# Four of eight experts in 96 places: 64 as column halves, 32 on four column tiles, plain float32 weights

## The chip, the cores and the metric

One core of one Trainium2 chip runs the kernel in one launch. The metric is device time in microseconds (us), the median of several runs. The engines are TensorE (PE; PEld is its weight load), VectorE (DVE), ScalarE (ACT), GpSimd (POOL) and SyncE (SP), whose queue issues the weight transfers.

## The reference, cut to what matters

A two-layer encoder trunk over 256 positions of width 1024, in float32. The change touches only the last sub-layer, in which each position goes through two of eight SwiGLU experts, 3584 wide:

```python
def moe_swiglu(h, w_router, w_gate, w_up, w_down):
    logits = (h @ w_router).astype(jnp.float32)
    top_v, top_i = lax.top_k(logits, TOP_K)          # 2 of 8
    gates = jax.nn.softmax(top_v, axis=-1)
    dense_gate = jnp.sum(jax.nn.one_hot(top_i, N_EXPERTS) * gates[..., None], axis=-2)
    y = jnp.zeros_like(h)
    for e in range(N_EXPERTS):
        y = y + dense_gate[..., e:e + 1] * swiglu(h, w_gate[e], w_up[e], w_down[e])
    return y
```

With the reference's own inputs its router gives the eight experts 70, 71, 46, 62, 84, 71, 66 and 42 positions.

## The kernel before, in words

Weights come from HBM in pieces of 128 partitions x 1024 floats (512 KB), issued by SP in one fixed order into a pool of `NW` = 34 such buffers. `Stream` keeps the account: `load` issues a transfer, `fill` issues as many as buffers allow (`NW - ROOM` alive at once), `step` turns a piece that is not marked `RAW` into two float32r pieces, `hi` (ACT, line 193) and `lo` = raw - hi (DVE, line 194), and `get` hands the pieces of a unit out, one k-slice at a time, ahead of the products that use them.

In the expert stage the experts are sorted by their number of positions. Rank 0 is always expert 0; ranks 1 to 7 are the others, smallest first. They are worked through in the order of `RANKS` = (0, 1, 7, 6, 2, 5, 4, 3). An expert's columns come in seven slices of 512 (`NFE`), and each slice has a gate product (`pg`), an up product (`pu`), both over 8 k-slices, and a down product (`y`), over 4 k-slices and two output halves. There are two forms:

- Ranks 0, 4, 5, 6, 7 hold 128 places. Each weight is split, and `mm3` (lines 362 to 364) issues three float32r products in place of one: hi x hi, hi x lo, lo x hi. A slice has 72 of them, 128 columns of TensorE and 512 moving elements wide: 24 for gate, 24 for up, 24 for down.
- Ranks 1, 2, 3 (`SMALL`) hold `PLACES` = 64 places. Their weights stay raw, and the products are plain float32, which show in the trace as two records (passes) each. TensorE's array is used as two column tiles of 64: two slices are taken at a time, one on each half (`halves_of`; lines 1158, 1190). A step is thus two slices, and the seventh slice a step of its own whose halves are 256 elements wide.

The main loop (from line 1338 on) issues for each step: gate, `Silu` on ACT (line 1382), up, the multiplication on DVE (line 1384), and then the down product of the step before. All engines run in the order of the program. Smaller work is put into this order by beats: `st.soon(n, fn)` calls `fn` after n more pieces were handed out. So come in between the products: the transposes of the activation (`act_T`, line 1169), the gather of the next expert's rows (`gather`, line 1080, from `expert_in`), the transposed selection matrix `ohT` (line 1126), and, once an expert is done, `expert_out` and four pieces of `scatter` (line 1237), two products each for the hi and lo part of the result, and one addition on DVE.

If an expert had more positions than places, an `overflow` branch behind the loop would work them off.

Of the kernel before, what the change touches and what calls it, by code (L numbers as in the profile page):

```python
# [21 lines left out]
P = 128  # L22
D = 1024
KD = D // P
# [11 lines left out]
SMALL = (1, 2, 3)  # L36
PLACES = 64
EXPERT = 12 * NFE
WINDOWS = (2, 4, 8, 16)
# [12 lines left out]
def trunk_(es, tc, stream, experts, blocks, x, xT, c, columns, ada_w, ln_g, ln_b, ev_w_in, pool_w, ev_sink, ev_w_out,  # L52
# [277 lines left out]
    def expert_units(stage, step):  # L330
        s, fs = step
        r = RANKS[s]
        if stage < 2:
            ks, what = [[(f * 12 + stage * 4 + u, 2) for u in range(4)] for f in fs], None
        elif fs[-1] == NFE - 1:

            ks, what = [[(fs[0] * 12 + 8 + n * 2 + u, 2) for u in range(2)] for n in range(2)], None
        else:
            ks, what = [[(f * 12 + 8 + u, 1) for u in range(4)] for f in fs], None
        if r in SMALL:  # L340
# [101 lines left out]
    with ExitStack() as ph:  # L442
# [423 lines left out]
        for g in range(1, NG):  # L866
            ffn_gu(g)
            if g == 1:
                at_once(next_x(z, affine_rows(0, 0)))

                earlier = cst.tile([P, NE, NE], F32, name="earlier")
                G.iota(earlier, pattern=[[1, NE], [-1, NE]], base=0, channel_multiplier=0, allow_small_or_imprecise_dtypes=True)
                G.tensor_scalar(earlier, earlier, 0.0, None, op0=ALU.is_gt)

                G.iota(upto, pattern=[[1, P]], base=0, channel_multiplier=-1, allow_small_or_imprecise_dtypes=True)
                G.tensor_scalar(upto, upto, 0.0, None, op0=ALU.is_ge)
                slot = cst.tile([P, P], F32, name="slot")
# [3 lines left out]
                G.memset(places[:, SMALL[0]:SMALL[-1] + 1], float(PLACES))  # L881
            if g == NG - 1:
# [179 lines left out]
    with ExitStack() as ph:  # L1062
# [27 lines left out]
        def expert_in(s, res):  # L1090
# [4 lines left out]
            here = (mA, mB)[s % 2]  # L1095
            if small:
                h = here.tile([P, KD, PLACES], F32, tag="hh", name="hs")
# [4 lines left out]
            res[:] = h, ohT  # L1102
            yield 10
            for q in range(2):
                sl = slice(q * 4, q * 4 + 4)
                ps = gather(oh, q, PLACES if small else P)
                yield 1
                if small:
                    affine(h[:, sl, :], ps, q)
                    yield 10  # L1110
                    continue
# [7 lines left out]
            if s == NE - 1:  # L1119
                ungated, oh = oh, m1.tile([P, NT, P], F32, tag="oh", name="og", bufs=2)  # L1120
                for t in range(NT):
                    V.tensor_scalar(oh[:, t, :], ungated[:, t, :], gate_by[:, t, r:r + 1], None, op0=ALU.mult)
                yield 2
            ps = pst.tile([P, 512], F32, tag="t", name="pso")
            for t in range(NT):
                T.transpose(ps[:, t * P:(t + 1) * P], oh[:, t, :], ident)
            yield 1
            A.activation(ohT, ps[:, 0:S], AF.Copy)

        def by_halves(stages):  # L1130
# [9 lines left out]
        def up_gate(step, h, ps):  # L1140
# [18 lines left out]
            for _ in ws:  # L1159
                pass  # L1160

        def act_T(step, act, res):

# [14 lines left out]
        def down(step, aT, y):  # L1178
            s, fs = step
            small = RANKS[s] in SMALL  # L1180
            if fs[-1] == NFE - 1:
                for n in range(2):
                    down_half(step, aT, y, n)
            elif small:
                ws = st.get()
                for kk in range(4):
                    pair = [next(ws) for _ in range(2)]
                    for n in range(2):
                        for rows_, w in zip(halves_of, pair):
                            T.matmul(y[n][rows_, :], lhsT=aT[0][:, kk, rows_], rhs=w[:, n * 512:(n + 1) * 512],  # L1190
                                     start=fs[0] == 0 and kk == 0, stop=False)
                for _ in ws:
                    pass
# [8 lines left out]
        def down_half(step, aT, y, n):  # L1202

            ws = list(st.get())
            if RANKS[step[0]] in SMALL:
                for k in range(2):
                    for b, rows_ in enumerate(halves_of):
                        T.matmul(y[n][rows_, :], lhsT=aT[0][:, k, rows_], rhs=ws[b * 2 + k], start=False, stop=k == 1)  # L1208
            else:
                for k, w in enumerate(ws):  # L1210
                    mm3(y[n], sl2(aT, lambda a: a[:, k, :]), w, False, k == 3)

        def expert_out(y, res):

            yhl = last8.tile([P, 2, D], F32R, tag="d", name="yhl")
            yh, yl = yhl[:, 0, :], yhl[:, 1, :]
            res[:] = yh, yl
            sls = [slice(n * 512, n * 512 + 512) for n in range(2)]
            yf = last4.tile([P, D], F32, tag="r", name="yf")
# [3 lines left out]
            for sl in sls:  # L1223
                A.activation(yh[:, sl], yf[:, sl], AF.Copy)
                yield 1
            for sl in sls:
                V.tensor_tensor(yl[:, sl], yf[:, sl], yh[:, sl], op=ALU.subtract)
                yield 1

        def scatter(r, ohT, ys):  # L1230

            for t in range(NT):
                for n in range(2):
                    sl = slice(n * 512, n * 512 + 512)
                    ps = pst.tile([P, 512], F32, tag="t", name="pssc")
                    for i, yy in enumerate(ys):
                        T.matmul(ps, lhsT=ohT[:, t * P:(t + 1) * P], rhs=yy[:, sl], start=i == 0,
                                 stop=i == len(ys) - 1)
                    yield 1
# [23 lines left out]
        def overflow(r, base):  # L1263
# [3 lines left out]
            for q in range(2):  # L1267
                affine(h2[:, q * 4:q * 4 + 4, :], gather(oh, q), q)
            y = [psa.tile([P, 512], F32, tag="b", name="y2") for _ in range(2)]
            for f in range(NFE):  # L1270
                gu = []
                for w in range(2):
# [5 lines left out]
                    gu.append(ps)  # L1278
                act = m2.tile([P, 512], F32, tag="act", name="act2")
                A.activation(act, gu[0], AF.Silu)  # L1280
# [31 lines left out]
        cur = [None, None]  # L1312
        at_once(expert_in(0, cur))
        by_rank = cst.tile([P, 6, NE], F32, name="by_rank")
        pos_by, gate_by = by_rank[:, 0:2, :], by_rank[:, 2:4, :]
# [36 lines left out]
        for i, step in enumerate(steps):  # L1352
# [10 lines left out]
            if step == (0, (5,)):  # L1363
                cnt = nc.values_load(found[:, NE:NE + 1], min_val=0, max_val=S)
                by_halves(next_x(z, rows10))
            if (s, fs[0]) == (1, 2):
                for t in range(NT):
# [4 lines left out]
            aT = [None, None]  # L1372
            n = 256 if RANKS[s] in SMALL and len(fs) == 1 else 512
# [7 lines left out]
            act = m2.tile([P, 512], F32, tag="act", name="act")  # L1381
            A.activation(act[:, 0:n], pg[:, 0:n], AF.Silu)  # L1382
            up_gate(step, h, pu)
            V.tensor_tensor(act[:, 0:n], act[:, 0:n], pu[:, 0:n], op=ALU.mult)  # L1384
            st.soon(1 if final else 2 if n == 256 else 6, lambda step=step, act=act, aT=aT: by_halves(act_T(step, act, aT)))
            if prev is not None:
                pstep, paT, pohT = prev
                if pstep[1][0] == 0:
                    y = [psy.tile([P, 512], F32, tag="y", name="y") for _ in range(2)]
                down(pstep, paT, y)  # L1390
                if pstep[1][-1] == NFE - 1:
# [7 lines left out]
        with tc.If(cnt > 0):  # L1399
            for r in range(NE):  # L1400
                for base in (PLACES, PLACES + P) if r in SMALL else (P,):
                    overflow(r, base)
# [3 lines left out]
        halves = [slice(n * 512, n * 512 + 512) for n in range(2)]  # L1406
        yf = [m2.tile([P, 512], F32, tag="act", name="yf") for _ in range(2)]
        s6 = [sml.tile([P, 2, 6], F32, tag="s6", name="s6") for _ in range(NT)]
# [100 lines left out]
```

## Time and profile before

| | us |
|---|---|
| median of 3 runs (lowest, highest) | 1317.96 (1314.96, 1318.4) |
| the profiled execution's own time | 1321.59 |
| its span, first to last instruction | 1319.8 |
| PE busy / DVE busy / ACT busy | 1284.6 / 923.1 / 664.7 |
| HBM read | 468.05 MB, 355 GB/s over the span |

The expert stage begins at about 440 us and ends at about 1305 us. A busy TensorE says little here: products are pipelined, the busy time of one covers the start of the next, and so the pace is read from the starts of successive records in the timeline.

### The profile page before, as it was taken

Reading aid. Unit: us, or ns where it says so; the run is one execution under the profiler, and the core shown is the slowest. Engines: PE = TensorE matmul, PEld = TensorE weight load, DVE = VectorE, ACT = ScalarE, POOL = GpSimd, SP = SyncE. Lnnn points to the kernel's source line nnn. Section 1 sums busy time; section 2 is a strip of 40 time slices with the busy share of each in tenths; the row PEclk is TensorE's granted clock in tenths of the full one; section 3 lists DMA queues with packets and bytes.
Section 4 is the critical chain, followed back from the end, with each engine's and each line's share of the span. In section 5 each row is a group of like instructions: output and inputs, shape, how many; then the busy total and the mean of one; then the engine's idle time right before and its main releaser. Section 6 shows DMA issues by size and latency. Waiting matters only on the chain. (4 is left out here: it accounts for less than half of the span.)

```text
span 1319.8 us, 19031 instructions
## 1 busy us (share of the span) xinstructions
PE 1284.6 (97%) x6392; PEld 930.2 (70%) x6392; DVE 923.1 (70%) x1140; ACT 664.7 (50%) x840; POOL 15.5 (1%) x73
## 2 busy tenths in 40 slices
PE   6999999999999999999999999999999999999996
PEld 4758999996976788544688888854467888886332
DVE  7696999947865989312888898842089889975302
ACT  0416353526326777212678777832177777774100
POOL 1000000000000000000000000000000000000001
PEclk9999999999899999999999999999999999999998
DMA  9999899993782889999999999999999999999993
GB/s 372 408 409 367 302 346 356 366 350 129 265 339 106 285 304 347 392 409 409 409 408 409 409 409 353 337 387 409 408 409 409 409 409 409 350 330 372 410 409 142
DMA packets 129579, 470.46 MB, mean 356 GB/s; under 512 B 14520, under 2 KB 14656, under 8 KB 129472
## 3 DMA queue, kind: packets, MB, share of 16 engines
q1 hardware_dynamic: 129168, 468.89, 92.2%
q8 instruction: 52, 0.85, 0.3%
q14 instruction: 55, 0.45, 0.1%
q10 hardware_dynamic: 304, 0.27, 0.1%
HBM read 468.05 MB, written 1.05 MB: 355 GB/s over the span
## 5 line engine op out<-in xcount | busy, mean ns | idle before, releaser
L194 DVE TENSOR_TENSOR lo<-raw,hi 128x1024 fp32r<-128x1024 f32 x494 | 590.4, 1222 | 108.1 <-ACT hi L193 85.1
L193 ACT ACTIVATE hi<-raw 128x1024 fp32r<-128x1024 f32 x494 | 502.7, 1054 | 146.1 <-PE y L364 20.9
L269 DVE CUSTOM_DVE_ANT_0 raw<-raw,cond,colt 128x1024 f32<-128x1024 f32 x96 | 118.7, 1281 | 7.8 <-DMA raw<-in_stream 7.8
L363 PE MATMUL pu<-lo,hh 128*128 128x512 f32 x280 | 111.3, 397 | 1.2 <-DVE over L1344 1.0
L362 PE MATMUL y<-hi,ah 128*128 128x512 f32 x280 | 112.3, 401 | 0.0
L364 PE MATMUL y<-hi,al 128*128 128x512 f32 x280 | 111.0, 397 | 1.1 <-DVE al L1176 1.1
L362 PE MATMUL pu<-hi,hh 128*128 128x512 f32 x280 | 111.5, 398 | 0.0
L363 PE MATMUL y<-lo,ah 128*128 128x512 f32 x280 | 111.0, 396 | 0.1
L364 PE MATMUL pu<-hi,hl 128*128 128x512 f32 x280 | 111.0, 396 | 0.0
L362 PE MATMUL pg<-hi,hh 128*128 128x512 f32 x272 | 110.7, 407 | 0.0
L363 PE MATMUL pg<-lo,hh 128*128 128x512 f32 x272 | 107.9, 397 | 0.7 <-DVE lo L194 0.7
L364 PE MATMUL pg<-hi,hl 128*128 128x512 f32 x272 | 107.7, 396 | 0.0
L1384 DVE TENSOR_TENSOR act<-act,pu 128x512 f32<-128x512 f32 (+1 forms) x47 | 31.3, 666 | 100.0 <-PE pu L1158 92.4
L1174 ACT ACTIVATE ah<-psT 128x512 fp32r<-128x512 f32 (+2 forms) x47 | 27.1, 578 | 133.6 <-PE psT L1169 133.3
L362 PE MATMUL psgu<-hh,hi 128*128 128x256 f32 x320 | 90.3, 282 | 0.0
L364 PE MATMUL psgu<-hh,lo 128*128 128x256 f32 x320 | 90.1, 282 | 0.0
L363 PE MATMUL psgu<-hl,hi 128*128 128x256 f32 x320 | 89.6, 280 | 0.0
L1158 PE MATMUL pu<-raw,hs 128*64 128x512 f32 (+1 forms) x384 | 76.6, 542 | 0.0
L1158 PE MATMUL pg<-raw,hs 128*64 128x512 f32 (+1 forms) x384 | 75.8, 542 | 0.0
L1382 ACT ACTIVATE act<-pg 128x512 f32<-128x512 f32 (+1 forms) x47 | 27.4, 583 | 84.6 <-PE pg L1158 62.3
L1190 PE MATMUL y<-raw,ah 128*64 128x512 f32 x288 | 66.4, 597 | 0.2 <-DMA raw<-in_experts 0.2
L363 PEld LDWEIGHTS pu<-lo,hh 128*128 128x128 f32 x280 | 52.7, 188 | 14.9 <-DVE over L1344 1.4
(274 smaller groups left out, 1822.8 us busy)
## 6 DMA issues: line engine op xcount, KB each, us to landing
raw<-in_experts SPq DMA_DIRECT2D x668, 512.0 KB, 10.1
raw<-in_stream SPq DMA_DIRECT2D x204, 512.0 KB, 7.9
lng<-in_ln_g SPq DMA_DIRECT2D x4, 512.0 KB, 7.5
lnb<-in_ln_b SPq DMA_DIRECT2D x4, 512.0 KB, 8.3
xT<-in_xT SPq DMA_DIRECT2D x2, 512.0 KB, 7.7
x<-in_x SPq DMA_DIRECT2D x2, 512.0 KB, 10.2
guest<-in_experts SPq DMA_DIRECT2D x2, 512.0 KB, 10.1
guests<-in_experts SPq DMA_DIRECT2D x2, 512.0 KB, 6.9
```

The lines of the kernel that those rows point to most:

```text
L193: A.activation(hi, raw, AF.Copy)
L194: V.tensor_tensor(lo, raw, hi, op=ALU.subtract)
L269: V.tensor_tensor_reduce(raw[:, 0, :], raw[:, 0, :], cond, 1.0, adab[:, i:i + 1], ALU.mult, ALU.add, accum_out=mod[l, part][:, kk:kk + 1])
L362: T.matmul(ps, lhsT=l[0], rhs=r[0], start=start, stop=False)
L363: T.matmul(ps, lhsT=l[0], rhs=r[1], start=False, stop=False)
L364: T.matmul(ps, lhsT=l[1], rhs=r[0], start=False, stop=stop)
L1158: T.matmul(ps[rows_, 0:w.shape[-1]], lhsT=h[:, kk + k, :], rhs=w, start=kk + k == 0, stop=kk + k == KD - 1)
L1174: A.activation(ah[:, 0:n, :], ps[:, 0:n, :], AF.Copy)
L1190: T.matmul(y[n][rows_, :], lhsT=aT[0][:, kk, rows_], rhs=w[:, n * 512:(n + 1) * 512], start=fs[0] == 0 and kk == 0, stop=False)
L1382: A.activation(act[:, 0:n], pg[:, 0:n], AF.Silu)
L1384: V.tensor_tensor(act[:, 0:n], act[:, 0:n], pu[:, 0:n], op=ALU.mult)
```

## The change

Ranks 4 to 7 (`MIDDLE`) get 96 places, and take the raw form with two slices per step. Their first 64 places go as those of the small experts do, on two column tiles of 64. The other 32 (`MORE`) go on four column tiles of 32, which take the two slices of up and the two of gate at once (`pm`), and in the down product two slices times two output halves (`ym`). All four weight pieces of a step's k-pair are drawn ahead of its products. Their activation is transposed apart (`psTm`), and their result, whose four blocks have to be summed, is scattered by two further products per piece with two selection matrices `ohM` (`more` times `quarters`). Rank 0 stays as it was. The pool of weight buffers shrinks from 34 to 30.

```diff
+MIDDLE = (4, 5, 6, 7)
+MORE = 32
...
-    NW = 34
+    NW = 30
...
+        if r in MIDDLE and stage < 2:
+            if stage == 0:
+                st.add_expert(r, [(f * 12 + w * 4 + u, 2) for u in range(4) for w in range(2) for f in fs], RAW)
+            return
...
-             (((0, 1), (2, 3), (4, 5), (6,)) if RANKS[s] in SMALL else [(f,) for f in range(NFE)])]
+             (((0, 1), (2, 3), (4, 5), (6,)) if RANKS[s] in SMALL + MIDDLE else [(f,) for f in range(NFE)])]
...
+        def both(step, h, pg, pu, pm):
+            s, fs = step
+            ws = st.get()
+            for kk in range(0, KD, 2):
+                w = [next(ws) for _ in range(4 * len(fs))]
+                for k in range(2):
+                    if len(fs) == 2:
+                        g, u = (w[k], w[2 + k]), (w[4 + k], w[6 + k])
+                    else:
+                        g, u = ((a[:, 0:S], a[:, S:2 * S]) for a in (w[k], w[2 + k]))
+                    n = g[0].shape[-1]
+                    flags = dict(start=kk + k == 0, stop=kk + k == KD - 1)
+                    for ps, pair in ((pg, g), (pu, u)):
+                        for rows_, a in zip(halves_of, pair):
+                            T.matmul(ps[rows_, 0:n], lhsT=h[:, kk + k, 0:PLACES], rhs=a, **flags)
+                    for b, a in enumerate(u + g):
+                        T.matmul(pm[b * MORE:(b + 1) * MORE, 0:n], lhsT=h[:, kk + k, PLACES:], rhs=a, **flags)
...
+        def act_T_both(step, act, actm, res):
...
+            for k in range(n):
+                T.transpose(ps[:, k, :], act[:, k * P:(k + 1) * P], ident)
+            yield 1
+            A.activation(ah[:, 0:n, :], ps[:, 0:n, :], AF.Copy)
...
+            for k in range(n):
+                T.transpose(ps[:, k, :], actm[0:2 * MORE, k * P:(k + 1) * P], ident[0:2 * MORE, 0:2 * MORE])
+            yield 1
+            V.tensor_copy(am[:, 0:n, :], ps[:, 0:n, :])
...
+        def down_more(am, k, b, w, y, first, last):
+            for n, a in w:
+                q = b * 2 + n
+                T.matmul(y[q * MORE:(q + 1) * MORE, :], lhsT=am[:, k, b * MORE:(b + 1) * MORE], rhs=a, start=first, stop=last)
...
+                    if RANKS[s] in MIDDLE:
+                        for b, w in enumerate(pair):
+                            down_more(aT[1], kk, b, [(n, w[:, n * 512:(n + 1) * 512]) for n in range(2)], y[2],
+                                      fs[0] == 0 and kk == 0, False)
...
         def down_half(step, aT, y, n):
...
+                    if RANKS[step[0]] in MIDDLE:
+                        for b in range(2):
+                            down_more(aT[1], k, b, [(n, ws[b * 2 + k])], y[2], False, k == 1)
...
         def scatter(r, ohT, ys):
...
+                    oT, oM = ohT if isinstance(ohT, tuple) else (ohT, None)
+                    ops = [(oT, yy[:, sl]) for yy in ys[:2]]
+                    if oM is not None:
+                        ops += [(oM[:, n, :], ys[2][:, i, :]) for i in range(2)]
...
-            pu = psa.tile([P, 512], F32, tag="b", name="pu")
+            pu = psa.tile([P, 512], F32, tag="b", name="pu", bufs=1)
...
+            elif RANKS[s] in MIDDLE:
+                pm = psa.tile([P, 512], F32, tag="a", name="pm")
+                both(step, h, pg, pu, pm)
...
+            if RANKS[s] in MIDDLE:
+                actm = m2.tile([P, 512], F32, tag="act", name="actm", bufs=3)
+                half = slice(0, 2 * MORE)
+                A.activation(actm[half, 0:n], pm[2 * MORE:, 0:n], AF.Silu)
+                V.tensor_tensor(act[:, 0:n], act[:, 0:n], pu[:, 0:n], op=ALU.mult)
+                V.tensor_tensor(actm[half, 0:n], actm[half, 0:n], pm[half, 0:n], op=ALU.mult)
+                st.soon(2 if n == 256 else 4, lambda step=step, act=act, actm=actm, aT=aT: by_halves(act_T_both(step, act, actm, aT)))
```

How the change moves TensorE's work shows in the order of its instructions. In the gate product of rank 7's second slice (the third expert in line), TensorE has before, with the transposes of the first slice's activation (`psT`) put in between:

```order
L362 MATMUL pg<-hi,hh 128x512
L363 MATMUL pg<-lo,hh 128x512
L364 MATMUL pg<-hi,hl 128x512
L1169 MATMUL psT<-ident,act 128x128 x4
L362 MATMUL pg<-hi,hh 128x512
```

The first three rows make one k-slice of one slice's gate, and all of it is 128 columns wide. At the same place, in the first and second step of rank 7, TensorE now has (`64x512` and `32x512` are 64 and 32 columns of the array; the `y` rows are the last down products of the small expert before):

```order
L1207 MATMUL pm<-raw,hs 32x512 x4
L1285 MATMUL y<-raw,ah 64x512 x4
L1219 MATMUL psT<-ident,act 128x128 x4
L1285 MATMUL y<-raw,ah 64x512 x4
L1224 MATMUL psTm<-ident,actm 128x64 x4
L1205 MATMUL pg<-raw,hs 64x512 x2
L1205 MATMUL pu<-raw,hs 64x512 x2
L1207 MATMUL pm<-raw,hs 32x512 x4
L1205 MATMUL pg<-raw,hs 64x512 x2
L1205 MATMUL pu<-raw,hs 64x512 x2
L1207 MATMUL pm<-raw,hs 32x512 x4
```

One k-slice of gate and up, for two slices of columns, is now two pairs at 64 columns and four products at 32, and with each k-slice the tile goes from 64 to 32 and back. What is put in between is 128 columns wide, or, for `psTm`, 64 rows. In the down product of rank 7's first step there stands, from the end of the scatter of the expert before on:

```order
L1331 MATMUL pssc<-yhl,ohT 128x512 x2
L1263 MATMUL y<-raw,ah 64x512 x4
L1233 MATMUL ym<-raw,am 32x512 x4
L1263 MATMUL y<-raw,ah 64x512 x4
L1233 MATMUL ym<-raw,am 32x512 x4
L1219 MATMUL psT<-ident,act 128x128 x4
L1088 MATMUL psg<-oh,z 128x96 x8
L1224 MATMUL psTm<-ident,actm 128x64 x4
L1263 MATMUL y<-raw,ah 64x512 x4
L1233 MATMUL ym<-raw,am 32x512 x4
```

The same alternation, once per k-slice, takes the place of the down rows `L362 MATMUL y<-hi,ah 128x512` and their two fellows. Over the whole program the shape of TensorE's tile changes 88 times from one product to the next before, and 512 times now: 192 times from 64 to 32 columns, 160 times straight back, and 160 times otherwise.

## Rows read from the trace of the kernel before

**Rows 1.** TensorE, DMA and clock by stretch of the expert stage: us, busy (xinstructions), PEclk, DMA share, GB/s.
```profile
core 0: us, PE busy (x) PEld busy (x) DVE busy (x) ACT busy (x) POOL busy (x), PEclk, DMA share, GB/s
...
629.00:656.00 27.00, 26.93 (x118) 19.26 (x117) 21.97 (x23) 19.37 (x21) 0.00 (x0) 1.00 1.03 409
...
710.00:737.00 27.00, 27.00 (x129) 22.07 (x128) 22.53 (x22) 20.26 (x27) 0.00 (x0) 1.00 1.03 409
818.00:845.00 27.00, 27.00 (x130) 22.15 (x129) 20.41 (x19) 20.65 (x27) 0.00 (x0) 1.00 0.91 322
...
1142.00:1169.00 27.00, 27.00 (x130) 22.20 (x129) 22.16 (x21) 21.59 (x27) 0.00 (x0) 1.00 0.93 319
1223.00:1250.00 27.00, 27.00 (x118) 11.20 (x114) 10.38 (x13) 5.52 (x7) 0.00 (x0) 1.00 1.03 409
1250.00:1277.00 27.00, 27.00 (x127) 8.93 (x126) 1.87 (x3) 1.19 (x2) 0.00 (x0) 1.00 1.03 409
```

**Rows 2.** What the load queue on SP waited for, whole run: us, times, longest.
```profile
SPq L157 <- DMA raw<-in_experts: 307.5, 419, 2.2
SPq L157 <- PE y L364: 117.6, 67, 8.5
...
SPq L157 <- PE pu L364: 76.7, 63, 11.2
```

**Rows 3.** What TensorE waited for, expert stage: us, times, longest.
```profile
PEld pg L1158 <- DMA raw<-in_experts: 3.5, 12, 0.4
...
PEld y L1190 <- DMA raw<-in_experts: 2.8, 7, 1.1
...
PEld y L362 <- ACT hi L193: 2.4, 3, 0.8
...
PEld pg L362 <- ACT hi L193: 1.6, 2, 0.8
...
PE y L364 <- DVE al L1176: 1.1, 1, 1.1
...
PEld y L363 <- DVE lo L194: 0.7, 2, 0.5
```

**Rows 4.** Timeline, split products of a 128-place expert: start us, us, what.
```profile
747.39 0.39 PE L362 MATMUL pg<-hi,hh 128*128 128x512 f32 x1
747.63 0.39 PE L363 MATMUL pg<-lo,hh 128*128 128x512 f32 x1
...
749.97 0.40 PE L364 MATMUL pg<-hi,hl 128*128 128x512 f32 x1
750.21 0.60 PE L1169 MATMUL psT<-ident,act 128*128 128x128 f32 x4
```

**Rows 5.** Timeline, plain float32 products on all 128 columns.
```profile
81.58 10.89 PE L715 MATMUL y<-raw,yT 128*128 128x512 f32 x25
```

**Rows 6.** Timeline, a 64-place expert: pairs of products on column halves, with transposes between.
```profile
604.07 0.66 PE L1169 MATMUL psT<-ident,act 128*128 128x128 f32 x4
604.66 1.94 PE L1190 MATMUL y<-raw,ah 128*64 128x512 f32 x8
606.43 3.62 PE L1158 MATMUL pg<-raw,hs 128*64 128x256 f32 x32
609.88 3.62 PE L1158 MATMUL pu<-raw,hs 128*64 128x256 f32 x32
613.33 1.89 PE L1190 MATMUL y<-raw,ah 128*64 128x512 f32 x8
615.15 0.44 PE L1169 MATMUL psT<-ident,act 128*128 128x128 f32 x2
615.52 5.37 PE L1190 MATMUL y<-raw,ah 128*64 128x512 f32 x24
```

**Rows 7.** Timeline, change between products of 8 and 128 rows.
```profile
350.25 1.12 PE L949 MATMUL pssv<-bs,ident 8*128 8x256 f32 x4
351.30 1.16 PE L953 MATMUL pssv<-wsT,vn 128*128 128x128 f32 x8
352.39 1.12 PE L949 MATMUL pssv<-bs,ident 8*128 8x256 f32 x4
```

**Rows 8.** Size of a weight transfer.
```profile
raw<-in_experts SPq DMA_DIRECT2D x668, 512.0 KB, 10.1
```

More of the change, by code (lines that the diff above doesn't have):

```diff
@@ L1095, in expert_in @@
             here = (mA, mB)[s % 2]
-            if small:
-                h = here.tile([P, KD, PLACES], F32, tag="hh", name="hs")
+            middle = r in MIDDLE
+            n = PLACES if small else PLACES + MORE if middle else P
+            if small or middle:
+                h = here.tile([P, KD, n], F32, tag="hh", name="hs")
             else:
@@ L1101, in expert_in @@
             ohT = m1.tile([P, S], F32 if s == NE - 1 else F32R, tag="ohT", name="ohT", bufs=2)
-            res[:] = h, ohT
+            if middle:
+                ohM = m1.tile([P, 2, S], F32R, tag="ohM", name="ohM", bufs=2)
+            res[:] = h, (ohT, ohM) if middle else ohT
             yield 10
@@ L1105, in expert_in @@
                 sl = slice(q * 4, q * 4 + 4)
-                ps = gather(oh, q, PLACES if small else P)
+                ps = gather(oh, q, n)
                 yield 1
-                if small:
+                if small or middle:
                     affine(h[:, sl, :], ps, q)
@@ L1123, in expert_in @@
                 yield 2
+            if middle:
+                oh = select(pos_by, r, 0, m1.tile([P, NT, P], F32, tag="oh", name="oh", bufs=2), True)
+                more = m1.tile([P, NT, P], F32, tag="oh", name="more", bufs=2)
+                for t in range(NT):
+                    V.tensor_scalar(more[:, t, :].rearrange("p (b n) -> p b n", b=4),
+                                    slot[:, PLACES:PLACES + MORE].unsqueeze(1).to_broadcast([P, 4, MORE]), 0.0,
+                                    pos_by[:, t, r:r + 1], op0=ALU.add, op1=ALU.is_equal)
+                yield 2
             ps = pst.tile([P, 512], F32, tag="t", name="pso")
@@ L1126, in expert_in @@
                 T.transpose(ps[:, t * P:(t + 1) * P], oh[:, t, :], ident)
+            if middle:
+                for t in range(NT):
+                    T.transpose(ps[:, S + t * P:S + (t + 1) * P], more[:, t, :], ident)
             yield 1
             A.activation(ohT, ps[:, 0:S], AF.Copy)
+            if middle:
+                for n in range(2):
+                    A.activation(ohM[:, n, :], ps[:, S:2 * S], AF.Copy, scale=quarters[:, n:n + 1])
         def by_halves(stages):
@@ L1160, in up_gate @@
                 pass
+        def both(step, h, pg, pu, pm):
[15 more added lines that the diff above has]
+                        T.matmul(pm[b * MORE:(b + 1) * MORE, 0:n], lhsT=h[:, kk + k, PLACES:], rhs=a, **flags)
+            for _ in ws:
+                pass
+        def act_T_both(step, act, actm, res):
+            n = 2 if len(step[1]) == 1 else 4
+            ah = ma.tile([P, 4, P], F32, tag="ah", name="ah")
+            am = ma.tile([P, 4, 2 * MORE], F32, tag="al", name="am")
+            res[:] = ah, am
+            ps = pst.tile([P, 4, P], F32, tag="t", name="psT")
+            for k in range(n):
+                T.transpose(ps[:, k, :], act[:, k * P:(k + 1) * P], ident)
+            yield 1
+            A.activation(ah[:, 0:n, :], ps[:, 0:n, :], AF.Copy)
+            ps = pst.tile([P, 4, 2 * MORE], F32, tag="t", name="psTm")
+            for k in range(n):
[6 more added lines that the diff above has]
+                T.matmul(y[q * MORE:(q + 1) * MORE, :], lhsT=am[:, k, b * MORE:(b + 1) * MORE], rhs=a, start=first, stop=last)
         def act_T(step, act, res):
@@ L1179, in down @@
             s, fs = step
-            small = RANKS[s] in SMALL
+            small = RANKS[s] in SMALL + MIDDLE
             if fs[-1] == NFE - 1:
@@ L1204, in down_half @@
             ws = list(st.get())
-            if RANKS[step[0]] in SMALL:
+            if RANKS[step[0]] in SMALL + MIDDLE:
                 for k in range(2):
@@ L1217, in expert_out @@
             res[:] = yh, yl
+            if len(y) == 3:
+                yq = m1.tile([P, 2, 512], F32R, tag="yq", name="yq")
+                res.append(yq)
             sls = [slice(n * 512, n * 512 + 512) for n in range(2)]
@@ L1225, in expert_out @@
                 yield 1
+            if len(y) == 3:
+                ym = m2.tile([P, 512], F32, tag="hf", name="ym")
+                V.tensor_tensor(ym, y[2], gtm, op=ALU.mult)
+                yield 1
+                A.activation(yq[:, 0, :], ym, AF.Copy)
             for sl in sls:
@@ L1235, in scatter @@
                     ps = pst.tile([P, 512], F32, tag="t", name="pssc")
-                    for i, yy in enumerate(ys):
-                        T.matmul(ps, lhsT=ohT[:, t * P:(t + 1) * P], rhs=yy[:, sl], start=i == 0,
-                                 stop=i == len(ys) - 1)
+                    oT, oM = ohT if isinstance(ohT, tuple) else (ohT, None)
+                    ops = [(oT, yy[:, sl]) for yy in ys[:2]]
+                    if oM is not None:
+                        ops += [(oM[:, n, :], ys[2][:, i, :]) for i in range(2)]
+                    for i, (l, yy) in enumerate(ops):
+                        T.matmul(ps, lhsT=l[:, t * P:(t + 1) * P], rhs=yy, start=i == 0, stop=i == len(ops) - 1)
                     yield 1
@@ L1268, in overflow @@
                 affine(h2[:, q * 4:q * 4 + 4, :], gather(oh, q), q)
-            y = [psa.tile([P, 512], F32, tag="b", name="y2") for _ in range(2)]
+            y = [psa.tile([P, 512], F32, tag="b", name="y2", bufs=1), psy.tile([P, 512], F32, tag="m", name="y2", bufs=1)]
             for f in range(NFE):
@@ L1278, in overflow @@
                     gu.append(ps)
-                act = m2.tile([P, 512], F32, tag="act", name="act2")
+                act = m2.tile([P, 512], F32, tag="act", name="act2", bufs=3)
                 A.activation(act, gu[0], AF.Silu)
@@ L1313, in trunk_ @@
         at_once(expert_in(0, cur))
+        quarters = cst.tile([P, 2], F32, name="quarters")
+        for q in range(4):
+            for n in range(2):
+                G.memset(quarters[q * MORE:(q + 1) * MORE, n:n + 1], float(q % 2 == n))
+        gtm = cst.tile([P, 512], F32, name="gtm")
         by_rank = cst.tile([P, 6, NE], F32, name="by_rank")
@@ L1365, in trunk_ @@
                 by_halves(next_x(z, rows10))
+            if step == (0, (4,)):
+                for q in range(4):
+                    A.activation(gtm[q * MORE:(q + 1) * MORE, :], gt[q * MORE:(q + 1) * MORE, q % 2 * 512:q % 2 * 512 + 512],
+                                 AF.Copy)
             if (s, fs[0]) == (1, 2):
@@ L1372, in trunk_ @@
             aT = [None, None]
[L1373 removed]
+            n = 256 if RANKS[s] in SMALL + MIDDLE and len(fs) == 1 else 512
             pg = psa.tile([P, 512], F32, tag="a", name="pg")
[L1375 removed]
+            pu = psa.tile([P, 512], F32, tag="b", name="pu", bufs=1)
             if i == 0:
@@ L1389, in trunk_ @@
                     y = [psy.tile([P, 512], F32, tag="y", name="y") for _ in range(2)]
+                    if RANKS[pstep[0]] in MIDDLE:
+                        y.append(psy.tile([P, 512], F32, tag="m", name="ym", bufs=1))
                 down(pstep, paT, y)
@@ L1400, in trunk_ @@
             for r in range(NE):
-                for base in (PLACES, PLACES + P) if r in SMALL else (P,):
+                for base in (PLACES, PLACES + P) if r in SMALL else (PLACES + MORE, PLACES + MORE + P) if r in MIDDLE else (P,):
                     overflow(r, base)
@@ L1406, in trunk_ @@
         halves = [slice(n * 512, n * 512 + 512) for n in range(2)]
-        yf = [m2.tile([P, 512], F32, tag="act", name="yf") for _ in range(2)]
+        yf = [m2.tile([P, 512], F32, tag="act", name="yf", bufs=3) for _ in range(2)]
         s6 = [sml.tile([P, 2, 6], F32, tag="s6", name="s6") for _ in range(NT)]
```

14 lines of the change are left out of this document (9 added, 5 removed).

## The prediction

> **What bounds the kernel now.** I looked first at the expert stage by stretches [rows 1], since all that the change touches is there. TensorE is busy for the whole of nearly every stretch, at a granted clock of 1.00, the upper level of 2.4 GHz. Memory is close behind: 409 GB/s in most stretches. But in the later half of each run of split experts it falls to 322 and 319 GB/s, and the reader is to see why: SP, which issues the transfers, then waits for products that free buffers, 117.6 us for `y` and 76.7 us for `pu` over the run [rows 2]. So there memory waits for TensorE. The other way round there is next to nothing: in the whole stage TensorE waits 3.5 and 2.8 us for landing weights [rows 3]. VectorE has 20 to 22 us of work in 27 where weights are split and 1 to 10 where they aren't, and what TensorE waits for the split comes to 2.4 + 1.6 + 1.1 + 0.7 = 5.8 us [rows 3]. TensorE's instruction stream is the bound. Busy time is no pace there (it is 27.00 of 27 whatever runs), so I read prices from differences of start times.
>
> - A split product: 11 intervals from 747.39 to 749.97, so 2.58 / 11 = 0.2345 us [rows 4].
> - A plain float32 pass on all 128 columns, 512 wide: 25 records in 10.89 us; one lasts 0.59, so 10.30 / 24 = 0.429 us [rows 5].
> - The same as pairs on column halves: 24 records take 5.37 and 8 take 1.94 us, both runs behind a transpose, so 16 records, eight pairs, take 3.43 us [rows 6]. That is 0.429 us for two products' pass: the halves run wholly side by side. A product has two passes, so a pair costs 0.858 us; at 256 wide (606.43 to 609.88, 16 pairs of records) 3.45 / 8 = 0.431 us.
> - A transpose: 0.66 us for four and 0.44 us for two [rows 6], so 0.11 us each.
> - A change of the tile's shape. From 613.33 to 615.15 there are four passes (1.72 us) and 0.10 us more; from 615.15 to 615.52 two transposes (0.22) and 0.15 more; and the run of 24 that follows lasts 5.37 where 11 x 0.429 + 0.59 = 5.31 is due [rows 6]. Two changes, 64 to 128 columns and back, lose 0.31 us: 0.15 us each.
>
> **The change, part by part.** *Products.* Four experts lose 7 x 72 split products each, 2016 x 0.2345 = 472.8 us. I count what comes in groups, a group being a pair at 64 columns or a set of four at 32. A two-slice step has 8 k-slices of gate and up with 3 groups, and 4 of down with 3: 36 groups of 0.858 us. The last step has 24 groups of 256 width for gate and up, and 8 for down, four of which fill only two of the four tiles. An expert: (3 x 36 + 8) x 0.858 + 24 x 0.431 = 109.9 us, four experts 439.5 us. Together -33.3 us. This prices a set of four like a pair, 0.858 us. The trace has no tile of 32 columns; its bounds are 0.858 (all four side by side) and 1.716 us (two at a time, the most that any row shows). I take the lower, because going from one tile to two cost nothing at all [rows 5, 6], and keep the upper as a rival.
>
> *Tile changes.* The order of instructions has 512 in place of 88, so 424 more: 4 x 4 x (8 + 4) x 2 = 384 belong to the alternation of 64 and 32 columns (352 go straight, 32 return by way of a piece put in between), 40 to those pieces. No row has a change between 64 and 32. Bounds: nothing, if the array takes it as no change; 0.20 us, the dearest in the trace, between products of 8 and 128 rows (350.25 to 351.30 is 1.05 us for four passes of 0.216, 351.30 to 352.39 is 1.09 for eight of 0.11 [rows 7]). I take 0.15 us: it was that much for the narrower and for the wider tile alike, so it doesn't hang on the columns loaded. 424 x 0.15 = +63.6 us.
>
> *Scatter and selection.* Two more split products in each of four pieces, four experts: 32 x 0.2345 = 7.5 us. Two more transposes per expert for `ohM`: 8 x 0.11 = 0.9 us. Transposes of the activation stay equal in number (7 x 4 before, 14 + 14 now), and the gather keeps its 16 products. +8.4 us.
>
> *The split.* 336 ACT and 336 DVE instructions go. They lie beside TensorE's work; what they cost is the wait of 5.8 us above, of which four of five split experts give back some 4. Bounds 0 and -5.8; -4 us.
>
> *Buffers.* Four fewer hold back 4 x 512 KB [rows 8] at 409 GB/s, 5.1 us of transfers. TensorE is the slower side through split and 96-place experts, so the pool fills there either way. Where a 64-place expert eats the reserve, the trace shows waits of tenths of a us [rows 3], so a reserve near its end: between 0 and +5.1 us, once, behind rank 0; later the reserve is larger, as no `hi` and `lo` take buffers. 0.
>
> *New waits.* `both` waits for four pieces at once, but they were issued long before. `pm` shares two PSUM buffers with `pg`; between a step's last use and the next step's lie the 12 groups of a down product, 10 us. `psTm` waits for one more DVE product, and its reader comes a step later. Nothing, as long as TensorE is the slow side; DVE has the split's time free.
>
> Sum: -33.3 + 63.6 + 8.4 - 4 = +34.7 us. The profiled execution took 1321.6 us, so it becomes 1356; the median shown is 3.6 us below that execution, so the forecast is **1353 us**.
>
> On the uncertain term, what the rows show is 0.15 us for 64 to 128 columns [rows 6]; they are silent on 64 to 32. The Trainium skill, in "TensorEngine Tiling (Array Packing)", section Tiling Modes, says that a change of the tiling mode, and not only of the tile, drains TensorE, which speaks against this change: by that rule 64 to 32 is a change like the others and the sum stays at 1353 us, while a reading in which only the use of another tile changes would leave 352 of them out (1300 us, below).
>
> **The rivals.** *Narrow tiles follow each other free (faster).* The 32-column tiles lie inside the 64-column ones, so the array might need no emptying. The 352 changes straight between the two cost nothing: 352 x 0.15 = 52.8 us less, **1300 us**. It decides below 0.05 us per change, where the sum meets the time before. Against it: every change of shape in the trace, of columns or of rows, costs 0.15 to 0.2 us [rows 6, 7], in either direction. For it: only that this one isn't among them. Memory would allow it by its dips, in which it idles a fifth of the time [rows 1].
>
> *Four tiles don't run side by side (far slower).* The sets of four cost 144 x 0.858 + 32 x 0.431 = 137.3 us in the sum. With three at a time they take a third more, +46 us: 1399 us. With two, +137 us: **1490 us**. For it: no row has more than two records starting together. Against it: two cost no more than one [rows 5, 6]. The Trainium skill, in "TensorE: Matmul & The Clock Gate", Part 3, reports 3.07 times for four row tiles; an estimate from that page would stretch the sets by 4 / 3.07, +42 us, 1395 us. The trace shows the whole factor of 2 for two tiles, which the page's shortfall would not give.
>
> *The change doesn't do what it says.* If a rank had over 96 positions the overflow branch would run a whole expert more, at least 7 x 24 plain products of 0.858 us, 144 us. The router's largest count is 84, the small ranks hold 42, 46 and 62: no branch.
>
> **How the numbers follow.** The sum with a price of 0.10 to 0.20 us on the 352 changes, and 5 us of starvation, gives 1335 to 1371 us: chance 0.68. Free changes: 0.15. Tiles not side by side: 0.16. Overflow: 0.01. The range must leave out at most 0.2, so it takes in the first two: 1298 to 1371 us. A difference within 0.3% (4 us) is about what a measurement can't tell from none; it lies between the first two cases, at a price of 0.04 to 0.06 us, 0.03 taken from both. Faster 0.14, same 0.03, slower 0.83.
>
> **What would show it.** In the timeline, records of `pm` (32 columns) in fours that start within some 0.03 us of each other; from the last such start to the next `pg` 0.43 + 0.10 us. A two-slice step without inserted pieces should take 36 x 0.858 + 24 x 0.15 + transposes, near 36 us, where two slices take 144 x 0.2345 + 0.9 = 34.7 us now. DVE and ACT fall to a few us in 27 through ranks 4 to 7, and the dips of memory grow deeper, as TensorE frees buffers more slowly. Steps of 32 us would mean free changes; fours that start as two and two, steps of 41 us or more. TensorE waits of more than 10 us on landing weights would mean that the smaller pool was the mistake.

## The result and the profile after

| | before | after |
|---|---|---|
| median, us (lowest, highest; 4 runs each) | 1316.95 (1314.96, 1318.4) | 1350.01 (1347.92, 1355.2) |
| ratio, 95% interval | | 1.0258 (1.0223 to 1.0293) |
| profiled execution's own time / span | 1321.59 / 1319.8 | 1348.47 / 1346.7 |

The change makes the kernel 33 us slower. The forecast was 1353 us.

The page of the changed kernel, busy us (share of the span) xinstructions:

```profile
PE 1315.8 (98%) x7360; PEld 675.1 (50%) x7360; DVE 522.9 (39%) x812; ACT 323.1 (24%) x504; POOL 16.5 (1%) x82
```

VectorE is down from 923 us to 523 and ScalarE from 665 to 323, and the time has gone up: both had been beside the path. The stretches of the expert stage, those that answer to [rows 1] (same columns):

```profile
core 0: us, PE busy (x) PEld busy (x) DVE busy (x) ACT busy (x) POOL busy (x), PEclk, DMA share, GB/s
629.00:656.00 27.00, 27.00 (x152) 6.71 (x150) 4.67 (x9) 2.93 (x5) 0.00 (x0) 1.00 1.03 409
710.00:737.00 27.00, 27.00 (x204) 8.45 (x200) 1.79 (x3) 1.79 (x3) 0.00 (x0) 1.00 1.03 408
801.00:828.00 27.00, 27.00 (x156) 9.45 (x152) 3.96 (x6) 3.08 (x7) 0.00 (x0) 1.00 0.79 297
1152.00:1179.00 27.00, 27.00 (x154) 9.45 (x152) 4.35 (x8) 4.25 (x11) 0.00 (x0) 1.00 0.81 296
1233.00:1260.00 27.00, 27.00 (x134) 7.27 (x132) 1.38 (x2) 1.23 (x2) 0.00 (x0) 1.00 1.00 374
```

TensorE is busy for 27 of 27 us still, at the same granted clock. VectorE has 1 to 5 us of work where it had 20 to 22. Memory idles more than before: 297 and 296 GB/s at the bottom of the dips, where it was 322 and 319 [rows 1]. The load queue says for whom (us, times, longest):

```profile
SPq L159 <- PE pm L1207: 114.4, 41, 6.4
...
SPq L159 <- PE ym L1233: 66.3, 40, 4.5
```

It now waits for the 32-column products, as it did for the split ones [rows 2]. So TensorE is the bound as before and has become slower. Its timeline in the third step of rank 7 (start us, us, what):

```profile
702.32 0.44 PE L1147 MATMUL pso<-ident,oh 128*128 128x128 f32 x2
702.59 0.38 PE L1150 MATMUL pso<-ident,more 128*128 128x128 f32 x2
702.90 1.08 PE L1205 MATMUL pg<-raw,hs 128*64 128x512 f32 x4
703.81 1.03 PE L1205 MATMUL pu<-raw,hs 128*64 128x512 f32 x4
704.77 1.06 PE L1207 MATMUL pm<-raw,hs 128*32 128x512 f32 x8
705.76 1.08 PE L1205 MATMUL pg<-raw,hs 128*64 128x512 f32 x4
706.67 1.03 PE L1205 MATMUL pu<-raw,hs 128*64 128x512 f32 x4
707.63 1.07 PE L1207 MATMUL pm<-raw,hs 128*32 128x512 f32 x8
```

From 702.90 to 705.76 lies one k-slice of gate and up: 2.86 us. Its three groups would take 6 x 0.429 = 2.57 us; the two changes of tile shape cost the other 0.29, 0.145 us each. Against the 0.858 us of a group by itself, 0.91 us pass from `pg` to `pu`, the group behind a change, 0.96 from `pu` to `pm`, with a change in front of `pm`, and 0.99 from `pm` to `pg`, with one on either side. The eight records of `pm` take 1.06 to 1.07 us together, two passes: the four tiles of 32 do run side by side.

To find where the 33 us lie, one distance in each trace is of use: from the first product of rank 1 to the start of the last up product, which leaves out the front of the program, whose TensorE clock differs from run to run.

| from the traces, us | first `pg` of rank 1 | last `pu` | distance | against before |
|---|---|---|---|---|
| before | 535.18 | 1282.73 | 747.55 | |
| after | 531.42 | 1314.73 | 783.31 | +35.8 |

Behind it the end is 5 us shorter than before. Timeline of the end, before:

```profile
1282.73 3.62 PE L1158 MATMUL pu<-raw,hs 128*64 128x256 f32 x32
...
1293.77 1.93 PE L1190 MATMUL y<-raw,ah 128*64 128x512 f32 x6 [0.23 <-DMA raw<-in_experts]
1298.30 5.21 PE L1433 MATMUL total<-x,ident 128*128 128x512 f32 x8 [2.59 <-PEq L1399]
```

and after:

```profile
1314.73 3.62 PE L1185 MATMUL pu<-raw,hs 128*64 128x256 f32 x32
...
1319.32 7.09 PE L1263 MATMUL y<-raw,ah 128*64 128x512 f32 x32
1326.72 3.67 PE L1549 MATMUL total<-x,ident 128*128 128x512 f32 x8 [0.31 <-PEq L1515]
```

From the last `pu` to `total` there are 15.57 us before and 11.99 after, and the eight records of `total` take 5.21 and 3.67 us. Before, the last weights came late: the last six records of `y` wait 0.23 us for them, and only then does TensorE's sequencer reach the overflow branch that stands behind the products:

```profile
L1399 PEldq COMPARE_BRANCH  x1: 4139/4139/4139, 1293.8 to 1293.8; - x1
```

The branch keeps the sequencer for 4.1 us while 1.9 us of products are left to run; hence the 2.59 us in front of `total`. With a slower TensorE the weights have landed in time, and the branch, 3.8 us from 1322.0 on, lies almost wholly beside products that are still queued: 0.31 us. The 5.21 us of `total` before, against 3.67, go with TensorE's clock: 0.72 was granted from 1298 to 1304 us, behind that wait, and 1.00 for the `total` of the changed kernel.

### The profile page after: what moved, and what is told of

The parts are those of the page before. It is cut to its first block, busy times and chain, and to the rows that moved or that the text cites. A ratio compares the mean times of both kernels' runs of the same rounds, so it can differ in the third digit from the quotient of the medians.

```text
span 1346.7 us, 19701 instructions
## 1 busy us (share of the span) xinstructions
PE 1315.8 (98%) x7360; PEld 675.1 (50%) x7360; DVE 522.9 (39%) x812; ACT 323.1 (24%) x504; POOL 16.5 (1%) x82
## 5 line engine op out<-in xcount | busy, mean ns | idle before, releaser
L196 DVE TENSOR_TENSOR lo<-raw,hi 128x1024 fp32r<-128x1024 f32 x158 | 186.4, 1220 | 32.1 <-ACT hi L195 25.6
L195 ACT ACTIVATE hi<-raw 128x1024 fp32r<-128x1024 f32 x158 | 159.0, 1053 | 67.0 <-PE y L371 12.8
L1263 PE MATMUL y<-raw,ah 128*64 128x512 f32 x672 | 160.4, 602 | 0.3 <-DMA raw<-in_experts 0.2
L1205 PE MATMUL pg<-raw,hs 128*64 128x512 f32 (+1 forms) x512 | 125.5, 564 | 0.2 <-DMA raw<-in_experts 0.2
L1207 PE MATMUL pm<-raw,hs 128*32 128x512 f32 (+1 forms) x1024 | 122.7, 551 | 0.0
L1205 PE MATMUL pu<-raw,hs 128*64 128x512 f32 (+1 forms) x512 | 119.0, 539 | 0.4 <-DMA raw<-in_experts 0.3
L1263 PEld LDWEIGHTS y<-raw,ah 128*64 128x64 f32 x672 | 43.5, 136 | 91.1 <-issue 76.2
L1185 PE MATMUL pu<-raw,hs 128*64 128x512 f32 (+1 forms) x384 | 76.6, 542 | 0.0
L1185 PE MATMUL pg<-raw,hs 128*64 128x512 f32 (+1 forms) x384 | 75.4, 541 | 0.0
L1233 PE MATMUL ym<-raw,am 128*32 128x512 f32 x448 | 68.0, 605 | 0.0
L1205 PEld LDWEIGHTS pu<-raw,hs 128*64 128x64 f32 x512 | 36.9, 137 | 61.1 <-issue 52.8
L369 PEld LDWEIGHTS psgu<-hh,hi 128*128 128x128 f32 x320 | 60.7, 190 | 0.4
```

The lines of the kernel that those rows point to most:

```text
L195: A.activation(hi, raw, AF.Copy)
L196: V.tensor_tensor(lo, raw, hi, op=ALU.subtract)
L369: T.matmul(ps, lhsT=l[0], rhs=r[0], start=start, stop=False)
L1185: T.matmul(ps[rows_, 0:w.shape[-1]], lhsT=h[:, kk + k, :], rhs=w, start=kk + k == 0, stop=kk + k == KD - 1)
L1205: T.matmul(ps[rows_, 0:n], lhsT=h[:, kk + k, 0:PLACES], rhs=a, **flags)
L1207: T.matmul(pm[b * MORE:(b + 1) * MORE, 0:n], lhsT=h[:, kk + k, PLACES:], rhs=a, **flags)
```

## The experiments

Theory: the changes of tile shape between 64 and 32 columns, some 0.147 us each, are worth more than what the products save. Rivals: weights that land late, from the smaller pool or from drawing four pieces at once; the narrow tiles as such; the added scatter. Each run was made beside the kernel before on the same chip, where that took 1321 to 1322 us; ratios are to it. The two reorderings hold pieces of weights longer, so the stream's account frees them only behind their second use.

**Two k-slices grouped.** The 32-column products of two k-slices (and of two in the down product) are issued behind the 64-column ones of both:

```diff
-                    for b, a in enumerate(u + g):
-                        T.matmul(pm[b * MORE:(b + 1) * MORE, 0:n], lhsT=h[:, kk + k, PLACES:], rhs=a, **flags)
...
+                    wide.append((kk + k, tuple(u) + tuple(g), flags))
+                if (kk + 2) % 2 == 0:
...
+                    for k, four, flags in wide:
+                        for b, a in enumerate(four):
+                            T.matmul(pm[b * MORE:(b + 1) * MORE, 0:n], lhsT=h[:, k, PLACES:], rhs=a, **flags)
+                    wide = []
+                    st.free(held)
```

> Same products and transfers as the change, but two k-slices' pairs at 64 columns first, then their two sets of four at 32: the order has 324 changes of tile shape in place of 512. Theory (each change between 64 and 32 columns costs 0.147 us, as in the changed kernel's timeline): 188 x 0.147 = 27.6 us less than the change's 1350, so 1322 us. Rival (the loss is weights that land late, by the smaller pool or the larger draws): nothing of that is touched, 1347 to 1353 us. Rival (the sets of four disturb each other or the added scatter is the loss): 1347 to 1353 us as well.

Measured: 1324.93 us, ratio 1.0027 (1.0010 to 1.0043), against 1.0258 for the change. The distance from rank 1 to the last `pu` is 755.88 us, 27.4 us less than the change's; 27.4 / 188 = 0.146 us per change. The timeline there:

```profile
709.14 1.92 PE L1223 MATMUL pm<-raw,hs 128*32 128x512 f32 x16
711.00 1.08 PE L1215 MATMUL pg<-raw,hs 128*64 128x512 f32 x4
711.90 1.03 PE L1215 MATMUL pu<-raw,hs 128*64 128x512 f32 x4
712.76 1.03 PE L1215 MATMUL pg<-raw,hs 128*64 128x512 f32 x4
713.62 1.03 PE L1215 MATMUL pu<-raw,hs 128*64 128x512 f32 x4
714.58 1.92 PE L1223 MATMUL pm<-raw,hs 128*32 128x512 f32 x16
```

Only `pg` behind `pm` at 711.00 and `pm` behind `pu` at 713.62 still pay: 0.90 and 0.96 us to the next start; the two groups in the middle, which paid in the change, take 0.86.

**Four k-slices grouped.** The same with `(kk + 2) % 4` and all four k-slices of the down product.

> The same with four k-slices grouped, in the down product too: 248 changes. Theory: 264 x 0.147 = 38.8 us less than the change, 1311 us, some 6 us below the kernel before. On a straight line through the change and the version with two k-slices. Rival (late weights): no gain, or a loss, since up to 8 pieces are now held until their second use: 1350 us or more.

Measured: 1317.64 us, ratio 0.9979 (0.9962 to 0.9997). The distance is 746.74 us, 36.6 less than the change's, where 264 x 0.147 = 38.8 were expected. So three versions with the same products get faster with each change of shape that goes, which no rival explains; the last 76 gave 9.1 us, 0.120 us each, where 11.2 were due. Of the 2 us that are missing, 1.7 lie at the end of rank 1, where TensorE loses 5.8 us to late weights (4.1 with two k-slices), by the comparison that is made below for the change. Pieces are held longer in this version; that this is the reason was not tried.

**The pool alone.**

```diff
-    NW = 34
+    NW = 30
```

in the kernel before.

> The kernel before with 30 weight buffers in place of 34, nothing else. Theory: 0 to 5 us more than before (1317 to 1322 us), as TensorE is the slower side where the pool fills. Rival (the smaller pool is the mistake): 20 us more or above, 1337 us or more.

Measured: 1336.55 us, ratio 1.0119 (1.0095 to 1.0144), 15 us slower than the 1321.63 beside it: between the two, and against my theory of 0 to 5 us. What TensorE waited for in its expert stage, against [rows 3]:

```profile
PEld y L1190 <- DMA raw<-in_experts: 9.3, 14, 1.7
...
PEld pg L362 <- ACT hi L193: 4.3, 4, 1.3
...
PEld pg L363 <- DVE lo L194: 3.1, 4, 1.1
```

The waits for landing weights in the 64-place experts have grown from 2.8 to 9.3 us in `y` alone, and the split at the beginning of the next expert waits with them. In its timeline the last step of rank 1 takes 17.0 us from its first product to the next expert's, and that of rank 2 16.8, where it was 14.4 for both; with the two steps behind each, 4.2 and 4.4 us are lost. The kernel before needs its 34 buffers: its reserve is gone whenever a small expert ends. The profiled executions differ by 15.4 us. From the first product of rank 1 to the last `pu` it is 9.5 us, these 8.6 among them; from there to `total` 4.2 (19.79 us in place of 15.57), where the last weights are late again; behind that 1.5 less. In front of rank 1 it is 3.2 us, with a granted clock of 0.92 in place of 0.94 from 330 to 440 us; whether the pool has a part in these is not shown.

Whether this is in the changed kernel's loss too, its own timeline tells. The end of rank 1, the only 64-place expert that has the split form in front of it:

```profile
612.25 5.22 PE L1263 MATMUL y<-raw,ah 128*64 128x512 f32 x18
617.68 1.50 PE L1263 MATMUL y<-raw,ah 128*64 128x512 f32 x5 [0.21 <-DMA raw<-in_experts]
618.95 0.64 PE L1205 MATMUL pg<-raw,hs 128*64 128x512 f32 x1
...
621.61 2.26 PE L1205 MATMUL pu<-raw,hs 128*64 128x512 f32 x4 [0.30 <-DMA raw<-in_experts]
623.80 1.06 PE L1207 MATMUL pm<-raw,hs 128*32 128x512 f32 x8
```

and the end of rank 2, which has the raw form in front:

```profile
970.88 5.37 PE L1263 MATMUL y<-raw,ah 128*64 128x512 f32 x24
976.08 1.03 PE L1205 MATMUL pg<-raw,hs 128*64 128x512 f32 x4
976.94 1.03 PE L1205 MATMUL pu<-raw,hs 128*64 128x512 f32 x4
977.90 1.07 PE L1207 MATMUL pm<-raw,hs 128*32 128x512 f32 x8
```

From the first record of `y` to that of `pm`, over the same 24 records and the next two groups, there are 11.55 us at the end of rank 1 and 7.02 at the end of rank 2. 4.5 us are lost there, once, and no later product of the stage starts late for weights: a raw piece takes one buffer where a split one takes two, so that 30 are enough for ranks 4 to 7.

The view that [rows 3] are from seems to say more. In the changed kernel's expert stage it has:

```profile
PEld y L1263 <- DMA raw<-in_experts: 13.5, 19, 1.1
...
PEld pg L1205 <- DMA raw<-in_experts: 7.8, 16, 1.1
...
PEld pu L1205 <- DMA raw<-in_experts: 2.7, 7, 1.0
```

That is 24 us, where [rows 3] have 6.3. But PEld is the weight load, which goes on beside the products before; time is lost only where a product starts late, and by the starts it is the 4.5 us.

**A smaller reserve in the changed kernel.** Only in the expert stage:

```diff
         st.guest(2)
-        st.ROOM = 4
+        st.ROOM = 8
```

> The change with four more buffers kept back in the expert stage alone (26 pieces alive less 4, in place of 26). Theory: TensorE waits for weights only where a 64-place expert has eaten the reserve; 1.28 us per missing piece at the end of rank 1, up to 5.1 us, and up to 3 us more at the ends of ranks 2 and 3: 1350 to 1358 us. Rival (the pool, not the changes of shape, makes the loss): as much again as the first four buffers, 20 us or more.

Measured: 1355.26 us, ratio 1.0252 (1.0218 to 1.0286), the change's own within the interval; the distance is 786.85 us, 3.5 longer, all of it at the end of rank 1, where 8.1 us are lost in place of 4.5. Four more buffers gone make a few us, not twenty: the pool doesn't carry the loss of the changed kernel.

**No added scatter.** The results of the places from 64 on are left out of the output:

```diff
-                    if oM is not None:
+                    if False:
```

> The change without the 32 added products of the scatter, so that the results of the places 64 to 95 are left out of the output; all else runs. Theory: 32 x 0.2345 = 7.5 us less, 1342 us. Rival (the added pieces cost more than their products, by waits on what expert_out now does): 15 us less or more, below 1335 us.

Measured: 1344.33 us, ratio 1.0175 (1.0146 to 1.0205); distance 775.26 us, 8.1 less than the change's, where the products alone were put at 7.5. No waits hang on them.

**Thirty-two columns throughout.** The same 96 places, but the first 64 go as two tiles of 32 each, with the same moving data:

```diff
-                        for rows_, a in zip(halves_of, pair):
-                            T.matmul(ps[rows_, 0:n], lhsT=h[:, kk + k, 0:PLACES], rhs=a, **flags)
+                        for q in range(4):
+                            T.matmul(ps[q * MORE:(q + 1) * MORE, 0:n],
+                                     lhsT=h[:, kk + k, q % 2 * MORE:(q % 2 + 1) * MORE], rhs=pair[q // 2], **flags)
```

and so in the down product.

> The change with its 64-column products cut in two each, so that ranks 4 to 7 run on four column tiles of 32 throughout: per k-slice three sets of four in place of two pairs and a set of four, the same 0.858 us each, but no change of shape inside a product. The order has 170 changes in place of 512. Theory: 342 x 0.147 = 50 us less than the change, 1300 us, 0.987 of the kernel before. Rival (what costs is the narrow tile itself, not the change from 64 to 32): no gain or a loss, 1350 us and up. Rival (sets of four with four different weights slow each other): fours here share their moving data two and two, so a gain over 50 us.

Measured: 1302.88 us, ratio 0.9868 (0.9839 to 0.9897). It is the fastest so far, 1.3% faster than the kernel before, with more instructions than the change. Distance 733.20 us, 50.1 less than the change's: 50.1 / 342 = 0.147 us per change. The timeline at the same place:

```profile
702.08 1.04 PE L1208 MATMUL pm<-raw,hs 128*32 128x512 f32 x8
702.93 1.04 PE L1205 MATMUL pg<-raw,hs 128*32 128x512 f32 x8
703.79 1.04 PE L1205 MATMUL pu<-raw,hs 128*32 128x512 f32 x8
704.65 1.04 PE L1208 MATMUL pm<-raw,hs 128*32 128x512 f32 x8
```

From `pm` to `pm` 2.57 us, six passes of 0.429 and nothing besides. This decides against the narrow tile as the cause, and it takes the loss away without touching the pool, the scatter, the draws or the number of groups.

**Both output halves of the last step together.** Two versions, on the 32-column one and on that with four k-slices grouped: the last step's down product draws both halves' pieces, so that its sets of four are full.

```diff
+            if fs[-1] == NFE - 1 and RANKS[s] in MIDDLE:
+                held = []
+                two = [list(st.get(held)) for n in range(2)]
...
+                    for b in range(2):
+                        down_more(aT[1], k, b, [(n, two[n][b * 2 + k]) for n in range(2)], y[2], False, k == 1)
+                st.free(held)
```

> As the version with 32 columns throughout, and the down product of the last step takes both output halves together, so that its sets of four are full: 16 half-filled groups become 8 full ones, 8 x 0.858 = 6.9 us less. Theory: 1293 us, 0.982 of before. Rival (by now memory is the slower side): no gain over the version without it.

Measured: 1304.77 us, ratio 0.9876 (0.9848 to 0.9904): no gain over 0.9868. Its stretches (columns as above):

```profile
629.00:656.00 27.00, 26.75 (x222) 8.35 (x226) 4.62 (x9) 2.94 (x5) 0.00 (x0) 1.00 1.03 408
818.00:845.00 27.00, 27.00 (x254) 8.45 (x250) 1.79 (x3) 2.17 (x4) 0.00 (x0) 1.00 1.03 408
1142.00:1169.00 27.00, 27.00 (x254) 8.18 (x250) 1.37 (x2) 1.57 (x3) 0.00 (x0) 1.00 1.02 404
1223.00:1250.00 27.00, 27.00 (x122) 9.80 (x120) 3.69 (x5) 1.19 (x2) 0.00 (x0) 1.00 1.02 404
1250.00:1277.00 27.00, 26.41 (x157) 11.43 (x155) 1.11 (x2) 1.96 (x4) 0.00 (x0) 1.00 1.03 408
```

Memory runs at 404 to 408 GB/s in all of them, also where it had dipped to 322 and 319 [rows 1]. Its end:

```profile
1274.14 6.76 PE L1288 MATMUL y<-raw,ah 128*64 128x512 f32 x26
1282.01 1.93 PE L1288 MATMUL y<-raw,ah 128*64 128x512 f32 x6 [1.11 <-DMA raw<-in_experts]
1285.72 3.67 PE L1574 MATMUL total<-x,ident 128*128 128x512 f32 x8 [1.78 <-PEq L1540]
```

TensorE waits 1.11 us for weights and then 1.78 in front of `total`, for the branch. The distance, 731.39 us, is only 1.8 us shorter than without the regrouping, in place of 6.9, and from the last `pu` to `total` there are 16.17 us in place of 13.85. Memory is the slower side, as the rival had it; what TensorE gains, it waits.

> Four k-slices grouped as measured before (0.9979 of the kernel before), with the last step's down product taking both output halves together. 8 groups of 0.858 us and 8 changes of 0.147 us fewer, 8.1 us: 0.992 of the kernel before, 1309 us.

Measured: 1313.54 us, ratio 0.9945 (0.9924 to 0.9966), 0.0034 or 4.5 us below the version without it in place of 8.1. The distance, 740.65 us, is 6.1 us shorter; the end is longer again, as TensorE comes nearer to memory.

## Why the prediction was right

**The bound.** TensorE was the bound and stayed it. 336 instructions less on each of ACT and DVE gave little back, and memory's dips grew deeper, as foretold.

**The split, -4 us.** The 5.8 us that it was taken from are mostly waits of the weight load, which need not delay a product, and 1.1 of them belong to rank 0, which stays split. By the starts of TensorE's products, it waits for VectorE twice between rank 1 and the last `pu`, in stretches where VectorE has 25 and 26 us of work in 27:

```profile
659.36 0.73 PE L1237 MATMUL pssc<-yhl,ohT 128*128 128x512 f32 x2 [1.44 <-DVE x L1240]
...
997.23 0.73 PE L1237 MATMUL pssc<-yhl,ohT 128*128 128x512 f32 x2 [0.69 <-DVE x L1240]
```

Both are gone in the changed kernel: -2.1 us.

**Products, -33.3 us.** The uncertain part was whether four tiles run side by side. They do: a group of four takes two passes of 0.429 us, in the change as in the version with 32 columns throughout. The rival in which they don't (1399 to 1490 us) falls.

**Tile changes, +63.6 us.** The rows had 0.15 us for a change between 64 and 128 columns and none between 64 and 32; I took the same. Measured were 0.145 us in the timeline, 0.146 and 0.147 us by two of the experiments (0.139 with four k-slices, where more is lost to late weights); 424 x 0.146 = 61.9 us. So the rival with free changes (1300 us) falls too. The 32-column version, in which 10 of the 352 changes straight between the two are left, came out near its time (1302.88 us), and shows what that rival was worth.

**Scatter, +8.4 us.** The products of it (7.5) measured 8.1 us; the transposes (0.9) were not measured by themselves. Those of the activation, which were left out as equal in number, got cheaper: four of `psTm`, with 64 rows, take 0.38 us to the start of the next product (649.17 to 649.55), where four of `psT` take 0.59 [rows 6], so 0.05 us less each, and 56 of them some 2.8 us.

**Buffers, 0, between 0 and +5.1 us once behind rank 0.** 4.5 us in the place named, near the upper bound, where I took 0. But the reason that I gave, that TensorE is the slower side and the pool fills either way, holds for raw weights alone: in the kernel before, the same four buffers cost 15 us. And the sign that I had given for a mistaken pool, over 10 us of waiting on landing weights, did come, with 24 us in the view of [rows 3], though the pool costs 4.5: I should have tied it to the starts of products.

**The sum.** It was +34.7 us, and from rank 1 to the last `pu` it is 35.8 us longer. With the measured prices it would be -33.3 + 61.9 + 9.0 - 2.1 - 2.8 + 4.5 = +37.2, so 1.4 us stay unexplained. The medians differ by 33.1. Two things outside the sum make the profiled pair differ by less: TensorE reached rank 1 3.8 us earlier, where the program is nearly the same and the granted clock from 330 to 440 us was 0.97 in place of 0.94 (it was 0.92 to 0.97 over the traces of this study, so that looks like chance), and the end is 5 us shorter, which I had not seen: a kernel that ends on its last weights gives some of a slowdown back there.

That two terms decide, the products and the changes, and what each is worth, was right. That the forecast lies within 3 us of the median is in part luck: what made it too low (the buffers at nothing, too much back from the split) and what made it too high (the changes, the transposes, the end) nearly cancel. The range has a slip: 1371 us is the price of 0.20 us alone, and with the 5 us of starvation named beside it would be 1376.

## What to carry to other kernels

Count the changes of tile shape in the program's order and price them from any such change in the trace, here 0.15 us, before filling an array's idle columns with tiles of a second width: the filled columns saved 33 us and the changes took 62. Where work of two widths has to alternate, cut the wide tile into narrow ones, or group by width as far as buffers allow; the first costs nothing but instructions. Once the bound engine is quicker, look up which resource is next (here memory, at 404 to 409 GB/s) before removing more of its work. A wait of the weight load (PEld) is time lost only where a product then starts late, so waits are to be priced by the starts of products.

## What the runs showed that I had not expected

- Two 32-column products that share their moving data, each with its own 32 columns loaded, run beside two others at the full rate: eight records of `pg` in 1.04 us (the 32-column version). Halving the tile cost nothing here.
- A pool that is four buffers smaller cost the kernel before 15 us, three times my bound: its reserve is used up at the end of each small expert, and the split of the next expert's weights falls late with it.
- Filling the last half-empty groups gave nothing on the 32-column version, though TensorE shows 26.4 to 27 busy us of 27 in its stretches: busy time hides the waits for memory, and the flat GB/s show them.
